# Levels one to five of a triangular inverse as 64-row by 64-column quarters of the array

## The chip, the cores and the metric

One core of one Trainium2 chip runs the whole program. The metric is the device time of one execution in microseconds.

## What is computed

The reference is a network of two blocks: a first block with a gated delta rule mixer (GDN), a sparse attention mixer and two feed-forward stages, then a second block with an mLSTM, a grouped attention and a mixture of experts. The change lies in the GDN mixer. What matters of it, cut from the reference:

```python
def gated_delta_rule_chunked(q, k, v, g, beta):
    ...
    gc = jnp.cumsum(g, axis=-1)
    decay = jnp.where(incl, jnp.exp(gc[..., :, None] - gc[..., None, :]), 0.0)
    L = jnp.where(strict, jnp.einsum('bhnid,bhnjd->bhnij', k * beta, k) * decay, 0.0)
    T = triangular_solve(eye + L, eye, lower=True, unit_diagonal=True)
    u = jnp.einsum('bhnij,bhnjd->bhnid', T, v * beta[..., None])
    w = jnp.einsum('bhnij,bhnjd->bhnid', T, kb * jnp.exp(gc)[..., None])
    ...
```

There are 256 tokens and 8 heads of width 128. T is the inverse of a unit lower triangular matrix.

## The kernel before, in words

The kernel works on chunks of 128 tokens, so for each of the 8 heads there are two 128x128 inverses. `gdn` (called by `mixer`) makes four generators `gdn_pair`, one for each pair of heads, and steps them in turn, each new pair `GAP` = 6 steps behind the last. A pair has four problems (two heads, two halves of the tokens), held side by side in tiles of [128, 4, 128].

A pair first projects its q, k, v columns (`ws2`, lines 356 to 358, with the splits of the weights into a high and a low half at lines 412 and 413). It then builds the negated strict lower part (`NL`, tile EL) and the start of the inverse and its transpose (`x`, tile X, and `ti`, tile T). Six levels follow, for block sizes s = 2, 4, 8, 16, 32, 64. Each level has five steps on a chain:

1. four matmuls `py` = NL times the even blocks of ti (line 936), 64 columns each,
2. a copy of py to `y` by ScalarE (line 937),
3. four matmuls `pz` = x times y (line 939),
4. a predicated copy of pz into the even blocks of ti by VectorE (line 941), under a mask `dm`,
5. four transposes of ti (line 944) and a copy to x by ScalarE (line 945).

A 128x64 fp32 matmul of the program is two passes in the trace, each with its own weight load, so a group of four is eight MATMUL rows; a transpose is one pass. Tiles py, pz and px come from one PSUM pool of four buffers, each a bank.

The program gives no order of its own: a scheduler places each instruction on its engine's queue by dependencies, priorities and its own estimate of durations, and puts the projection matmuls of other pairs (called dense below) between the steps of a chain. Each engine then runs its queue in that order. The projections use `acc` PSUM tiles, which are a pool of their own.

Behind the inverse come the state recurrence of the pair, the memory attention (`mem_attn`), the output projection, and the rest of the network. Two other places use part of the array already: the 64-row matmuls of the grouped attention (line 1444, two heads at rows 0 and 64) and a matmul of 64 rows by 64 columns (line 1254).

Of the kernel before, what the change touches and what calls it, by code (L numbers as in the profile page):

```python
# [14 lines left out]
AF = mybir.ActivationFunctionType  # L15
# [286 lines left out]
class Net:  # L302
# [549 lines left out]
    def gdn_pair(self, u, X, pool, sp, gc, gl, epsc, ahead):  # L852

        nc, I = self.nc, self.I
        hs = slice(2 * u, 2 * u + 2)
        t = lambda name, shape, bufs=2: pool.tile([128] + shape, F32, name=name, bufs=bufs)
        mm = nc.tensor.matmul
# [7 lines left out]
        for j in (1, 0, 2):  # L865
            p, = self.ws2(ahead.pop(0) if ahead else I["gqkv"][4 * j + u], X)
# [35 lines left out]
        NL = AT = None  # L902
        for kind, row, msk, other in (("L", rL, "mstrict", kC), ("A", rA, "mincl", qC)):
# [11 lines left out]
            NL, AT = (e, None) if kind == "L" else (NL, e)  # L915
        yield
        x, y, ti = t("X", [4, 128]), t("Y", [4, 64]), t("T", [4, 128])
# [7 lines left out]
        dm = self.dm.bitcast(I32).rearrange("p (i c) -> p i c", i=6)  # L925

        def blocks(tile, s, odd):
            return tile.rearrange("p h (n two s) -> p h n two s", two=2, s=s)[:, :, :, odd, :]

        for lv in range(1, 7):  # L930
            s = 1 << lv
            n = 64 // s
            cut = lambda z: z.rearrange("p h (n s) -> p h n s", s=s)
            py, pz = self.pst([128, 4, 64]), self.pst([128, 4, 64])
            for i in range(4):
                mm(cut(py)[:, i], NL[:, i, :], blocks(ti, s, 0)[:, i], start=True, stop=True)
            nc.scalar.activation(y, py, AF.Copy)
            for i in range(4):
                mm(pz[:, i, :], x[:, i, :], y[:, i, :], start=True, stop=True)
            mk = dm[:, lv - 1, :].rearrange("p (n s) -> p n s", s=s)[:, None].to_broadcast([128, 4, n, s])  # L940
            nc.vector.copy_predicated(blocks(ti, s, 0), mk, cut(pz))
            px = self.pst([128, 4, 128])
            for i in range(4):
                nc.tensor.transpose(px[:, i, :], ti[:, i, :], ident)
            nc.scalar.activation(x, px, AF.Copy)
            yield
# [29 lines left out]
        pz = self.xs2(I["gz"][u], X)  # L976
# [905 lines left out]
```

## Time and profile before

| | |
|---|---|
| three runs, median (lowest to highest) | 2262.7 us (2260.46 to 2262.75) |
| the profiled execution, its own time | 2260.96 us |
| its span, first to last instruction | 2258.9 us |
| TensorE (PE) busy, weight loads (PEld) busy | 1943.6 us, 1362.3 us |
| VectorE (DVE) busy, ScalarE (ACT) busy | 1058.1 us, 770.9 us |
| first and last row of the inverse's matmuls | 60.0 us, 255.1 us |

Times in the profile are microseconds from the first instruction unless marked ns. PE rows are matmuls, PEld rows the weight loads that go beside them; a row's duration overlaps with the next one's, so the pace is read from starts, not durations. The name left of the arrow is what is written, right of it what is read. "128*64 128x256" means 128 rows by 64 columns of weights, and 256 moving columns. A row of the timeline with "x8" stands for eight neighbours; its duration runs from the first one's start to the last one's end.

### The profile page before, as it was taken

To read this page: it belongs to the slowest core of one execution; us is meant where nothing else is said; L and a number is where in the kernel's file an instruction comes from. 1 tells how busy PE (TensorE), PEld (TensorE's weight loads), DVE (VectorE), ACT (ScalarE), POOL (GpSimd) and SP (SyncE) were. 2 spreads that over 40 slices of the span, in tenths; PEclk is the share of its full clock that TensorE was granted. 3 is DMA by queue.
4 is the path that set the end of the run, shared out by engine and by line. 5 is a ranking of instruction groups with operands and counts; after the bars stand their busy time and mean duration, and the time that the engine had idled before them with its cause. 6 is when DMAs were issued, how large, how long until landed. Compare 5 with 4: busy or idle time off the path is not lost. (4 is left out here: it accounts for less than half of the span.)

```text
span 2258.9 us, 31633 instructions
## 1 busy us (share of the span) xinstructions
PE 1943.6 (86%) x12918; PEld 1362.3 (60%) x12919; DVE 1058.1 (47%) x1899; ACT 770.9 (34%) x1336; POOL 99.7 (4%) x137
## 2 busy tenths in 40 slices
PE   8999999999999999999987666767999996667665
PEld 7999889988987998877942111112778831112121
DVE  6555378774546987876541111101875531111011
ACT  6476555444555444655410000000745410000000
POOL 0001000000000000211100000000020000000000
PEclk9999999999999999999998888777999998887877
DMA  6322267865525886545799999999555799999997
GB/s 229 122 101 77 87 265 297 313 264 176 186 75 211 328 335 240 174 145 234 283 378 420 421 420 421 420 420 387 199 219 227 258 411 421 420 420 421 421 389 329
DMA packets 96401, 653.16 MB, mean 289 GB/s; under 512 B 11592, under 2 KB 14832, under 8 KB 18680
## 3 DMA queue, kind: packets, MB, share of 16 engines
q1 hardware_dynamic: 96248, 651.05, 73.3%
q8 instruction: 105, 1.72, 0.3%
q14 instruction: 48, 0.39, 0.0%
HBM read 649.93 MB, written 1.08 MB: 288 GB/s over the span
## 5 line engine op out<-in xcount | busy, mean ns | idle before, releaser
L413 DVE TENSOR_TENSOR whl<-raw,whl 128x1024 fp32r<-128x1024 f32 x342 | 422.1, 1242 | 154.7 <-ACT whl L412 154.0
L412 ACT ACTIVATE whl<-raw 128x1024 fp32r<-128x1024 f32 x342 | 359.9, 1057 | 318.1 <-PE acc L358 149.1
L1681 PE MATMUL mm<-raw,q_XT 128*32 128x512 f32 x1808 | 273.0, 712 | 115.0 <-DMA raw<-in_moe 114.8
L1674 ACT ACTIVATE q_XT<-mm,mc,modA 128x128 f32<-128x128 f32 x64 | 29.3, 458 | 589.8 <-DVE q_XT L1676 348.8
L1681 PEld LDWEIGHTS mm<-raw,q_XT 128*32 128x32 f32 x1808 | 46.6, 117 | 303.9 <-DMA raw<-in_moe 180.1
L357 PE MATMUL acc<-xl,whl 128*128 128x256 f32 x784 | 227.4, 291 | 0.8 <-DVE xl L571 0.7
L356 PE MATMUL acc<-xh,whl 128*128 128x256 f32 x784 | 225.8, 290 | 2.0 <-ACT whl L412 1.8
L358 PE MATMUL acc<-xh,whl 128*128 128x256 f32 x784 | 224.9, 288 | 0.5 <-DVE whl L413 0.5
L358 PE MATMUL mm<-xh,whl 128*128 128x256 f32 x704 | 200.7, 285 | 1.4 <-DVE whl L413 1.4
L356 PE MATMUL mm<-xh,whl 128*128 128x256 f32 x704 | 201.5, 286 | 0.3
L357 PE MATMUL mm<-xl,whl 128*128 128x256 f32 x704 | 200.9, 285 | 0.3 <-DVE xl L571 0.3
L357 PEld LDWEIGHTS acc<-xl,whl 128*128 128x128 f32 x784 | 151.3, 193 | 4.5 <-issue 2.1
L356 PEld LDWEIGHTS acc<-xh,whl 128*128 128x128 f32 x784 | 150.9, 193 | 4.8 <-ACT whl L412 2.7
L358 PEld LDWEIGHTS acc<-xh,whl 128*128 128x128 f32 x784 | 150.9, 193 | 2.4 <-issue 1.3
L356 PEld LDWEIGHTS mm<-xh,whl 128*128 128x128 f32 x704 | 136.4, 194 | 3.9 <-issue 2.5
L358 PEld LDWEIGHTS mm<-xh,whl 128*128 128x128 f32 x704 | 136.5, 194 | 1.9 <-DVE whl L413 1.8
L357 PEld LDWEIGHTS mm<-xl,whl 128*128 128x128 f32 x704 | 136.5, 194 | 1.5 <-DVE xl L571 0.7
L1681 PE MATMUL mm<-raw,q_aT 128*32 128x512 f32 x592 | 83.2, 649 | 32.3 <-DMA raw<-in_moe 28.5
L1715 DVE TENSOR_TENSOR q_y<-mm,gate 128x512 f32<-128x512 f32 x32 | 22.1, 692 | 185.6 <-PE mm L1681 185.6
L1704 DVE TENSOR_TENSOR q_a<-q_a,mm 128x512 f32<-128x512 f32 x16 | 11.0, 688 | 204.2 <-PE mm L1681 204.2
L1208 DVE SCALAR_TENSOR_TENSOR adas<-adaw,cond,adas 128x2048 f32<-128x2048 f32 x42 | 98.5, 2346 | 5.7 <-DMA adaw<-in_ada 5.7
L1717 PE MATMUL acc<-q_y,q_WT 128*128 128x512 f32 x128 | 78.0, 741 | 22.8 <-DVE q_y L1715 22.0
(547 smaller groups left out, 3392.5 us busy)
## 6 DMA issues: line engine op xcount, KB each, us to landing
raw<-in_moe SPq DMA_DIRECT2D x300, 1024.0 KB, 19.9
raw<-in_ffn SPq DMA_DIRECT2D x66, 1024.0 KB, 5.9
whl<-in_moe SPq DMA_DIRECT2D x56, 1024.0 KB, 19.8
adaw<-in_ada SPq DMA_DIRECT2D x48, 1024.0 KB, 8.8
raw<-in_gmga SPq DMA_DIRECT2D x16, 1024.0 KB, 4.9
rawxh<-in_moe SPq DMA_DIRECT2D x14, 1024.0 KB, 19.8
rawxl<-in_moe SPq DMA_DIRECT2D x14, 1024.0 KB, 19.8
raw<-in_gqkv SPq DMA_DIRECT2D x12, 1024.0 KB, 8.5
```

What stands on the lines that cost most here:

```text
L356: mm(out, lh, rh, start=start, stop=False)
L357: mm(out, lh, rl, start=False, stop=False)
L358: mm(out, ll, rh, start=False, stop=stop)
L412: i = self.nc.scalar.activation(hi, src, AF.Copy)
L413: return i, self.nc.vector.tensor_sub(lo, src, hi.bitcast(F32))
L1208: nc.vector.scalar_tensor_tensor(a, t, c, a, op0=OP.mult, op1=OP.add)
L1674: nc.scalar.activation(XT[:, k, :], p, AF.Identity, bias=B[:, k:k + 1], scale=A[:, k:k + 1])
L1681: mm(out[s, :], lhs[:, s], ut[:, 512 * e:512 * e + 512], start=start, stop=stop, tile_position=(0, 32 * e))
L1704: nc.vector.tensor_mul(a, a, gu[1])
L1715: nc.vector.tensor_mul(y, p, gate[:, h * 512:h * 512 + 512])
L1717: mm(accs[tt][h], WT[:, tt, :], y, start=first, stop=last)
```

## The change

For levels one to five a block of the next size (up to 64) lies inside one of the two diagonal 64x64 quarters of the 128x128 matrix. The change computes only these: each of the four matmuls becomes two, one on rows and columns 0 to 63 of the array, one on 64 to 127, with half the moving columns (32). The upper quarter's products lie in the tile that was py, the lower one's in the tile that was pz; the first 32 columns of each hold the first product, the other 32 the second. The copy of the first product is one ScalarE copy for the upper half and one VectorE copy for the lower, and the predicated copy is one for each half. Level six is as before. The changed program's lines are 942 and 951 for the matmuls of the quarters, 948 (ScalarE) and 946 (VectorE) for the copies, 955 for the predicated copies, 958 to 963 for level six, 966 and 967 for the transposes and their copy.

```diff
--- before.py
+++ after.py
@@ -932,13 +932,35 @@
             n = 64 // s
             cut = lambda z: z.rearrange("p h (n s) -> p h n s", s=s)
             py, pz = self.pst([128, 4, 64]), self.pst([128, 4, 64])
-            for i in range(4):
-                mm(cut(py)[:, i], NL[:, i, :], blocks(ti, s, 0)[:, i], start=True, stop=True)
-            nc.scalar.activation(y, py, AF.Copy)
-            for i in range(4):
-                mm(pz[:, i, :], x[:, i, :], y[:, i, :], start=True, stop=True)
-            mk = dm[:, lv - 1, :].rearrange("p (n s) -> p n s", s=s)[:, None].to_broadcast([128, 4, n, s])
-            nc.vector.copy_predicated(blocks(ti, s, 0), mk, cut(pz))
+            even = blocks(ti, s, 0)
+            if lv < 6:
+
+                m = n // 2
+                halves = [(p, slice(64 * j, 64 * j + 64), slice(m * j, m * j + m)) for j, p in enumerate((py, pz))]
+                for i in range(4):
+                    for p, r, c in halves:
+                        mm(cut(p)[r, i, :m], NL[r, i, r], even[r, i, c], start=True, stop=True,
+                           tile_position=(r.start, r.start))
+                for p, r, c in halves:
+                    if r.start:
+                        nc.vector.tensor_copy(y[r, :, :32], p[r, :, :32])
+                    else:
+                        nc.scalar.activation(y[r, :, :32], p[r, :, :32], AF.Copy)
+                for i in range(4):
+                    for p, r, c in halves:
+                        mm(p[r, i, 32:], x[r, i, r], y[r, i, :32], start=True, stop=True,
+                           tile_position=(r.start, r.start))
+                for p, r, c in halves:
+                    mk = dm[r, lv - 1, r.start // 2:r.start // 2 + 32].rearrange("p (n s) -> p n s", s=s)
+                    nc.vector.copy_predicated(even[r, :, c], mk[:, None].to_broadcast([64, 4, m, s]), cut(p)[r, :, m:])
+            else:
+                for i in range(4):
+                    mm(cut(py)[:, i], NL[:, i, :], even[:, i], start=True, stop=True)
+                nc.scalar.activation(y, py, AF.Copy)
+                for i in range(4):
+                    mm(pz[:, i, :], x[:, i, :], y[:, i, :], start=True, stop=True)
+                mk = dm[:, lv - 1, :].rearrange("p (n s) -> p n s", s=s)[:, None].to_broadcast([128, 4, n, s])
+                nc.vector.copy_predicated(even, mk, cut(pz))
             px = self.pst([128, 4, 128])
             for i in range(4):
                 nc.tensor.transpose(px[:, i, :], ti[:, i, :], ident)
```

How the order moves. TensorE, first pair, level one. mm_550 and mm_551 are py and pz, whl the splits, cath and catl the input of the projection. Before, from the first group to the second:

```order
L936 MATMUL mm_550<-T_541,EL_508 128x64 x4
L357 MATMUL acc_638<-catl_90,whl_663 128x256
L358 MATMUL acc_638<-cath_89,whl_663 128x256
L356 MATMUL acc_638<-cath_89,whl_663 128x256
L357 MATMUL acc_638<-catl_90,whl_663 128x256
L358 MATMUL acc_638<-cath_89,whl_663 128x256
L356 MATMUL acc_638<-cath_89,whl_663 128x256
L939 MATMUL mm_551<-Y_540,X_539 128x64 x4
```

Now, at the same place, from the end of the first group (L942, where mm_550 and mm_551 alternate):

```order
L942 MATMUL mm_551<-T_541,EL_508 64x32
L357 MATMUL acc_648<-catl_90,whl_673 128x256
L358 MATMUL acc_648<-cath_89,whl_673 128x256
L356 MATMUL acc_648<-cath_89,whl_673 128x256
L357 MATMUL acc_648<-catl_90,whl_673 128x256
L951 MATMUL mm_551<-Y_540,X_539 64x32 x4
L358 MATMUL acc_648<-cath_89,whl_673 128x256
L356 MATMUL acc_648<-cath_89,whl_673 128x256
L951 MATMUL mm_550<-Y_540,X_539 64x32 x4
```

The second group has moved up by two dense matmuls, and it is in two pieces: all four matmuls of the lower quarter, two dense matmuls, all four of the upper quarter.

TensorE, second pair, level two, where the first group is in two pieces. Before:

```order
L966 MATMUL mm_1249<-vT_263,X_539 128x128
L936 MATMUL mm_1255<-T_1194,EL_1143 128x64 x4
L356 MATMUL acc_1444<-xh_127,whl_1469 128x256
L357 MATMUL acc_1444<-xl_128,whl_1469 128x256
L358 MATMUL acc_1444<-xh_127,whl_1469 128x256
```

Now:

```order
L988 MATMUL mm_1309<-vT_263,X_539 128x128
L942 MATMUL mm_1315<-T_1244,EL_1193 64x32 x4
L358 MATMUL acc_1524<-xh_127,whl_1521 128x256
...
L358 MATMUL acc_1524<-xh_127,whl_1549 128x256
L942 MATMUL mm_1316<-T_1244,EL_1193 64x32 x4
L356 MATMUL acc_1524<-xh_127,whl_1549 128x256
L357 MATMUL acc_1524<-xl_128,whl_1549 128x256
```

Between the two quarters of one group now stand ten dense matmuls.

VectorE, first pair, level one. Before:

```order
L914 SCALAR_TENSOR_TENSOR EA_528<-mm_533,EA_528 128x512
L413 TENSOR_TENSOR whl_753<-raw_751,whl_753 128x1024
L941 COPY_PREDICATED T_541<-k_dm_239,mm_551 128x128x2
L413 TENSOR_TENSOR whl_768<-raw_751,whl_768 128x1024
L413 TENSOR_TENSOR whl_785<-raw_783,whl_785 128x1024
```

Now:

```order
L914 SCALAR_TENSOR_TENSOR EA_528<-mm_533,EA_528 128x512
L946 COPY Y_540<-mm_551 64x4x32
L413 TENSOR_TENSOR whl_763<-raw_761,whl_763 128x1024
L955 COPY_PREDICATED T_541<-k_dm_239,mm_550 64x4x16x2
L955 COPY_PREDICATED T_541<-k_dm_239,mm_551 64x4x16x2
L413 TENSOR_TENSOR whl_778<-raw_761,whl_778 128x1024
```

The lower quarter's copy of Y, which waits for the first group, now stands ahead of a split, and one predicated copy has become two.

## Rows read from the trace of the kernel before

**Rows 1.** The page: its first line, and TensorE's granted clock in 40 equal slices

```profile
span 2258.9 us, 31633 instructions
...
PEclk9999999999999999999998888777999998887877
```

**Rows 2.** Busy time by stretch: PE, PEld, DVE, ACT, POOL busy us (x count), clock, DMA share, GB/s

```profile
100.00:125.00 25.00, 24.95 (x215) 24.28 (x215) 16.39 (x37) 17.81 (x32) 0.83 (x1) 1.00 0.32 119
150.00:175.00 25.00, 24.92 (x218) 24.62 (x216) 17.59 (x37) 20.04 (x32) 0.02 (x1) 1.00 0.45 142
```

**Rows 3.** Groups by line, 50 to 260 us (last row: all of L1278)

```profile
L939 PE MATMUL mm<-Y,X 128*128 128x64 f32 x192 | 25.1, 273 | 0.0
...
L945 ACT ACTIVATE X<-mm 128x512 f32<-128x512 f32 x24 | 14.3, 595 | 24.0 <-PE mm L944 23.6
L941 DVE COPY_PREDICATED T<-k_dm,mm 128x256 f32<-128x256 int32 x24 | 11.8, 492 | 30.1 <-PE mm L939 30.0
...
L937 ACT ACTIVATE Y<-mm 128x256 f32<-128x256 f32 x24 | 9.2, 385 | 9.2 <-PE mm L936 9.0
...
L1278 DVE COPY lac<-mm x2: 274/275/276, 943.7 to 1610.9; 128x128 f32<-128x128 f32 x2
```

**Rows 4.** Timeline of PE, a group without a wait: start us, us, instruction

```profile
132.16 0.28 PE L358 MATMUL acc<-xh,whl 128*128 128x256 f32 x1
132.28 1.00 PE L939 MATMUL mm<-Y,X 128*128 128x64 f32 x8
133.09 0.36 PE L356 MATMUL acc<-xh,whl 128*128 128x256 f32 x1
133.29 0.28 PE L357 MATMUL acc<-xl,whl 128*128 128x256 f32 x1
```

**Rows 5.** The same, the first and the last of 14 groups that wait

```profile
59.77 0.28 PE L356 MATMUL acc<-cath,whl 128*128 128x256 f32 x1
60.02 1.11 PE L936 MATMUL mm<-T,EL 128*128 128x64 f32 x8
...
61.14 0.28 PE L358 MATMUL acc<-cath,whl 128*128 128x256 f32 x1
...
249.06 0.28 PE L358 MATMUL acc<-xh,whl 128*128 128x256 f32 x1
249.35 1.10 PE L939 MATMUL mm<-Y,X 128*128 128x64 f32 x8
250.27 0.36 PE L356 MATMUL acc<-xh,whl 128*128 128x256 f32 x1
250.47 0.28 PE L357 MATMUL acc<-xl,whl 128*128 128x256 f32 x1
```

**Rows 6.** PE around a 64-row group; last row: its first weight loads (PEld)

```profile
1027.14 0.28 PE L358 MATMUL acc<-xh,whl 128*128 128x256 f32 x1
1027.35 1.13 PE L1444 MATMUL mm<-akC,aqC 64*128 64x256 f32 x8
1028.41 0.39 PE L356 MATMUL acc<-xh,whl 128*128 128x256 f32 x1
...
1027.34 0.19 PEld L1444 LDWEIGHTS mm<-akC,aqC 64*128 64x128 f32 x2
```

**Rows 7.** PE around the 64x64 group; its weight loads; its durations in ns, min/median/max

```profile
933.29 0.64 PE L1254 MATMUL mm<-li,consts 64*64 64x256 f32 x2
933.87 0.39 PE L358 MATMUL acc<-xh,whl 128*128 128x256 f32 x1
934.09 0.28 PE L356 MATMUL acc<-xh,whl 128*128 128x256 f32 x1
...
933.29 0.19 PEld L1254 LDWEIGHTS mm<-li,consts 64*64 64x64 f32 x2 [0.20 <-ACT li L1252]
...
L1254 PEld LDWEIGHTS mm<-li,consts x4: 129/130/133, 933.3 to 1599.1; 64*64 64x64 f32 x4
L1254 PE MATMUL mm<-li,consts x4: 376/402/427, 933.3 to 1599.3; 64*64 64x256 f32 x4
```

## The prediction, made before the changed kernel ran

> **What bounds the kernel now.** I read the page's slices first, then busy time by stretch, then the chain's groups by line, then single groups on the timeline. The levels of the inverse run between about 60 and 255 us of a span of 2258.9 us, and the granted clock is 1.00 there, the 2.4 GHz level [rows 1, 2]. TensorE is busy 24.9 of 25 us in that stretch and DVE 16 to 18 [rows 2]: the stage is bound by TensorE, which is filled with split-precision projection matmuls ("dense", one every 0.12 us) while the chains of the four head pairs run between them. DVE and ACT wait for TensorE there, not the other way: the predicated copy (L941) waited 30.0 us for L939, the X copy (L945) 23.6 us for L944 [rows 3]. So a microsecond of TensorE time saved or added in the stage moves everything behind it by one. What stands behind it needs the residual stream that this stage produces, and the order of instructions there is the same in both kernels.
>
> **What a group costs now.** Four 128-row matmuls of 64 columns are eight passes, each with its own weight load. One group without a wait: last dense matmul at 132.16, group at 132.28, next dense at 133.09 and 133.29 [rows 4]. That is 1.13 us where two dense steps would take 0.24, so the group costs 0.89 us; each pass takes 0.112, the pace of a 128-column weight load. Of the 48 groups, 27 lie directly between dense matmuls. 13 of these cost 0.89 to 0.93. 14 wait first for their operand and cost 1.14 on the mean; the first and the last of them are shown (61.14 - 59.77 - 0.24 = 1.13 and 250.47 - 249.06 - 0.24 = 1.17) [rows 5]. In these the group itself is longer too: 0.92 from its start to the next dense matmul, against 0.81, because the first weight load could not be pulled ahead of the wait. Mean of the 27: 1.02. The change removes 40 groups (levels one to five, two groups, four pairs): 40 x 1.02 = **40.8 us**, of which 35.6 is the clean price.
>
> **What a quarter costs.** No row of the trace runs two 64x64 quarters with 32 columns. The nearest are 64-row groups. (a) Going in: dense at 1027.14, first 64-row matmul at 1027.35, so 0.21 instead of 0.12 [rows 6]; the weight load starts with it and was not pulled ahead. (b) First load: in the one 64-row by 64-column group two loads, 0.13 us each, take 0.19 together, so the second starts 0.06 after the first [rows 7]. (c) Coming out: that group's second matmul starts at 933.29 + 0.64 - 0.376 = 933.55, its 256 columns stream for 0.21, and the next dense matmul starts at 933.87, 0.1 after the stream's end; the dense one after it comes 0.22 later, not 0.12 [rows 7]. 32 columns would stream in 0.03, so last matmul to dense is 0.12. (d) A step: half the columns of the full group's load, half of 0.112 = 0.056; the ends are 0.03 (only the 32 columns count, the load is hidden) and 0.112 (no gain from fewer columns). I take 0.056, as (b) is the row of the same shape, and keep the ends for the rivals. Two quarters do load together: two 64-row loads of 0.18 us lie within 0.19 [rows 6]. A run of n steps then costs 0.21 + 0.06 + (n - 1) x 0.056 + 0.12 + 0.22 - 0.24 = 0.31 + 0.056 n; with n = 8 that is 0.76, against 0.89. 40 whole runs would cost 30.4 us, 5 less than the clean 35.6.
>
> The order does not keep them whole. In the first group of a level the two quarters alternate in 14 of 20 cases; four others run one quarter after the other with dense work between, and two break off one matmul early. In the second group only 6 of 20 are whole: in the other 14 one quarter goes as soon as its own copy of Y is due, then dense matmuls, then the other quarter. A half run has four matmuls of one quarter, eight passes one behind the other, so eight steps: the full 0.76. Counted through the whole order there are 61 runs with 466 steps (40 runs with 320 if all were whole): 61 x 0.31 + 466 x 0.056 = 18.9 + 26.1 = **45.0 us**.
>
> The Trainium skill, TensorEngine Tiling (Array Packing), section Key Properties, says that changing the tiling mode drains the engine; the 0.09 us in (a) and the 0.1 in (c) agree. The same page's section Theoretical Speedup gives up to 2x for a dimension of 64 or less; by it alone the 40 groups would halve, 17.8 us less, 2245, which is the first rival below.
>
> **Waits.** Of the 0.25 us that a waiting group costs more, 0.11 is the unhidden load, which a run has anyway (its 0.06), and up to 0.09 of the rest passes while the array drains. About 0.06 stays, on half of 40: 1.2 us. Y is copied by ACT and DVE side by side, 128 columns each: by the slope between 0.385 (256 columns) and 0.595 (512) an ACT copy is 0.28, a DVE copy of 128 columns 0.275 [rows 3], so 0.1 less per level. The predicated copy becomes two on the same engine, each between half of 0.49 and the whole; near 0.31 with the fixed part that these copies have, so 0.13 more per level [rows 3]. 20 levels: +0.6, hidden where dense work stands between; I take 0, bounds -2 and +3. DVE gets 20 x (0.275 + 0.62 - 0.49) = 8 us more work, which fits beside its 50 to 70% [rows 2]. But the Y copy on DVE waits for TensorE with a split (L413) queued behind it, whose low half TensorE itself needs; the split buffers are four deep, so I cost that at nothing, and at 5 us if that cover is gone. PSUM buffers: the same three per level, the first held until the predicated copy instead of the Y copy; within the same bounds. No DMA moves.
>
> **Sum.** 45.0 + 1.2 - 40.8 = **+5.4 us**. On the profiled execution (2260.96 us, with 2.1 us outside its span) that is 2266.4. The median of the three runs is 2262.7, 1.7 above it, and they spread over 2.3; on the median it is **2268.1**, which I give.
>
> **Rivals.** (1) The quarters pay. If going in and out cost nothing, the steps alone would be 466 x 0.056 = 26 us: 15 us less, 2248. It turns faster where the fixed part of a run is below 0.16 us (61 x 0.16 + 26.1 = 36, 4.5 under 40.8), or where a step is near 0.03 (18.9 + 14 = 33, 8 under). For it: more array in use. Against: both ways of the switch are seen [rows 6, 7], with the same prices. 0.04. (2) No change that shows: steps at 0.053, runs that end at transposes (whose identity loads faster) and no waits left, since a run takes longer and the copies are done: 45 - 2 + 0 - 40.8 = +2, 2265. For it: the switch hides waits. Against: it needs all of these at once, or a good part of them. 0.27. (3) Much slower: the two quarters do not load together, so that the 22 alternating runs take 16 steps, 22 x 8 x 0.056 = +10, 2278 (a step of 0.112 throughout would give +26, 2294); or DVE, blocked by its Y copies, starves TensorE of splits, +5 and more, 2273 to 2278. Against: loads side by side [rows 6] and the four buffers. 0.09. That the change does not do what it says is partly true already (half runs) and stands in the sum.
>
> **Numbers.** 0.2% (4.5 us) is about what a measurement of this kernel can tell from no change. My forecast, +4.5 to +9.5, has 0.60. With the third rival slower has 0.69, same 0.27, faster 0.04. The range, 2262.5 to 2275, takes in the bounds of the waits (-2, +3) and most of the second rival, and leaves out the first and most of the third.
>
> **What would show it.** TensorE busy as before between 60 and 255 us, and the last transposes of level six (L966) some 5 us later than 255. Between a dense matmul and the first quarter 0.21, from the last quarter matmul to the next dense 0.12, then 0.22; passes of one quarter 0.056 apart. Half runs of about 0.76 in excess. DVE busy some 8 us more. Wrong if quarter passes follow at less than 0.04 or at 0.11, if dense matmuls follow a quarter at their usual pace, or if TensorE shows new waits for the splits.

## The result and the profile after

| | before | changed |
|---|---|---|
| median of the runs (lowest to highest) | 2262.62 us (2260.46 to 2262.75) | 2274.07 us (2271.74 to 2278.85) |
| ratio, 95% interval | | 1.0053 (1.0036 to 1.007) |
| the profiled execution, its span | 2258.9 us | 2269.9 us |

The change made the kernel slower by 11.5 us on the medians; 5.4 was forecast, and the range to 2275 just holds the time. The same kernel measured once more, below, came to 2276.4, outside it.

The page of the changed kernel, its first line and the granted clock in 40 slices, to set beside [rows 1]:

```profile
span 2269.9 us, 32342 instructions
...
PEclk9999999999999999999998787877999997877778
```

Slices of 57 us hide what happened in the stage of the inverse. By stretches of 5 us (length; PE, PEld, DVE, ACT, POOL busy us; granted clock, DMA share, GB/s), the changed kernel:

```profile
100.00:105.00 5.00, 5.00 (x53) 4.60 (x53) 2.97 (x6) 0.59 (x2) 0.00 (x0) 0.89 0.47 192
105.00:110.00 5.00, 5.00 (x48) 4.32 (x46) 2.50 (x6) 3.97 (x6) 0.00 (x0) 0.77 0.01 3
...
245.00:250.00 5.00, 5.00 (x63) 4.46 (x61) 2.92 (x6) 2.28 (x4) 1.27 (x2) 1.00 0.00 0
250.00:255.00 5.00, 4.67 (x41) 3.72 (x40) 1.63 (x7) 3.33 (x5) 0.00 (x0) 0.91 0.01 3
255.00:260.00 5.00, 5.00 (x34) 4.61 (x34) 1.29 (x3) 1.50 (x4) 0.00 (x0) 0.50 0.00 0
260.00:265.00 5.00, 5.00 (x37) 4.71 (x37) 1.82 (x3) 1.51 (x2) 0.00 (x0) 0.57 0.20 25
```

The kernel before, in one of these stretches:

```profile
255.00:260.00 5.00, 4.98 (x37) 4.42 (x35) 0.00 (x0) 3.80 (x9) 0.04 (x1) 1.00 0.00 0
```

TensorE is still busy nearly all the time, so the stage is still bound by it. But it ran at the lower level (0.50, 1.2 GHz) for (0.11 + 0.23) x 5 / 0.5 = 3.4 us near 104 and for (0.09 + 0.50 + 0.43) x 5 / 0.5 = 10.2 us up to 264, where the kernel before had 1.00. That is 6.8 us of work lost, which the prediction did not foresee.

The groups by line, 50 to 270 us, beside [rows 3]; L942 and L951 are the quarters, L946 and L948 the copies of Y, L955 the predicated copies:

```profile
L951 PE MATMUL mm<-Y,X 64*64 64x32 f32 x320 | 23.2, 227 | 0.0
...
L942 PE MATMUL mm<-T,EL 64*64 64x32 f32 x320 | 17.2, 228 | 0.3
...
L955 DVE COPY_PREDICATED T<-k_dm,mm 64x128 f32<-64x128 int32 x40 | 13.0, 325 | 19.1 <-PE mm L951 14.2 <-ACT whl L412 2.4 <-issue 1.3
...
L946 DVE COPY Y<-mm 64x128 f32<-64x128 f32 x20 | 5.9, 294 | 29.7 <-PE mm L942 29.6
...
L948 ACT ACTIVATE Y<-mm 64x128 f32<-64x128 f32 x20 | 5.4, 269 | 4.3 <-PE mm L942 4.1
```

The copies cost what was estimated (0.269 for 0.28, 0.294 for 0.275, 0.325 for 0.31), and still the copies wait for TensorE. How a half run and a whole run look in the changed kernel, on the timeline of PE (start us, us, instruction), to set beside [rows 4]:

```profile
236.18 0.28 PE L358 MATMUL acc<-xh,whl 128*128 128x256 f32 x1
236.38 0.65 PE L951 MATMUL mm<-Y,X 64*64 64x32 f32 x8
236.96 0.39 PE L356 MATMUL acc<-xh,whl 128*128 128x256 f32 x1
237.18 0.28 PE L357 MATMUL acc<-xl,whl 128*128 128x256 f32 x1
...
247.69 0.28 PE L357 MATMUL acc<-xl,whl 128*128 128x256 f32 x1
247.90 0.66 PE L951 MATMUL mm<-Y,X 64*64 64x32 f32 x16
248.50 0.39 PE L358 MATMUL acc<-xh,whl 128*128 128x256 f32 x1
248.72 0.28 PE L356 MATMUL acc<-xh,whl 128*128 128x256 f32 x1
```

One pass is 0.22 us long (tile Y, instructions on PE; ns min/median/max, then first and last start):

```profile
L951 PE MATMUL mm<-Y,X x320: 219/219/313, 61.5 to 261.3; 64*64 64x32 f32 x160
```

The half run, eight passes of one quarter, costs 237.18 - 236.18 - 0.24 = 0.76 us; the whole run, sixteen passes of both, costs 248.72 - 247.69 - 0.24 = 0.79. So the second quarter is free when it goes beside the first (0.66 against 0.65 for the runs themselves), and a run that holds one quarter alone costs as much as one that holds both.

Where the time went is best read at a place behind the inverse at which both kernels do the same, the first L564 matmul on PE. Before, then changed:

```profile
305.87 0.60 PE L564 MATMUL acc<-diag,xres 128*128 128x128 f32 x4
```

```profile
320.20 0.60 PE L564 MATMUL acc<-diag,xres 128*128 128x128 f32 x4
```

The stage ends 14.3 us later. The same way of counting as above (second matmul behind a run, minus the last one before it, minus 0.24), summed over every run of the levels one to five, gives 50.0 us for the 61 runs of the changed kernel and 38.2 us for the 40 full groups before (46.2 for all 48, 8.0 of it level six): 11.9 more. Five runs lie at the low clock and took 6.6 us where five clean ones take 3.9. The other 6.8 - 2.7 = 4.1 us of lost clock fell on dense matmuls and transposes. Together 16.0; the remaining -1.7 is not traced to a place. Between 306 and 600 us 4.3 us come back. The kernel before had two low stretches there of 0.34 x 5 / 0.5 = 3.4 us each, which cost it 1.7 us of work each, and the changed one had none; that would be 3.4 of the 4.3 (kernel before, by stretch):

```profile
470.00:475.00 5.00, 2.73 (x23) 1.69 (x22) 5.00 (x8) 2.21 (x3) 0.00 (x0) 1.00 0.57 179
475.00:480.00 5.00, 5.00 (x30) 4.93 (x31) 3.82 (x4) 0.00 (x0) 0.00 (x0) 0.66 0.80 317
560.00:565.00 5.00, 3.89 (x67) 3.36 (x67) 0.93 (x3) 1.22 (x3) 0.19 (x1) 0.66 0.99 369
```

### The profile page after: what moved, and what is told of

It is laid out like the page before. It is cut to its first block, busy times and chain, and to the rows that moved or that the text cites. A ratio compares the mean times of both kernels' runs of the same rounds, so it can differ in the third digit from the quotient of the medians.

```text
span 2269.9 us, 32342 instructions
## 1 busy us (share of the span) xinstructions
PE 1969.6 (87%) x13238; PEld 1368.2 (60%) x13239; DVE 1067.9 (47%) x1939; ACT 768.2 (34%) x1336; POOL 94.3 (4%) x137
## 5 line engine op out<-in xcount | busy, mean ns | idle before, releaser
L1703 PE MATMUL mm<-raw,q_XT 128*32 128x512 f32 x1808 | 284.1, 737 | 110.2 <-DMA raw<-in_moe 110.1
L1723 DVE COPY q_WT<-mm 128x256 f32<-128x256 f32 x16 | 6.8, 423 | 195.6 <-PE mm L1721 195.6
```

The lines of the kernel that those rows point to most:

```text
L1703: mm(out[s, :], lhs[:, s], ut[:, 512 * e:512 * e + 512], start=start, stop=stop, tile_position=(0, 32 * e))
L1723: nc.vector.tensor_copy(WT, pt)
```

## The experiments

The theory: the quarters are cheap as such, and the change loses by how they are cut into runs. Each quarter has a PSUM tile of its own, so each becomes ready by its own copy, and the order sends it alone. Rivals: the evacuation (copies on two engines, two predicated copies), the PSUM buffers, the bank itself, and the clock.

In the table, runs are the pieces that the order makes of the 40 groups of levels one to five, the sum is that of their prices in the profile, counted as above, and L564 is when the first of these matmuls starts. Each ratio is to the kernel before in the same set of runs; its medians in the three sets are in the first row.

| kernel | runs | sum, us | L564 at, us | median, us | ratio (95%) |
|---|---|---|---|---|---|
| before | 45 | 38.2 | 305.9 | 2262.5 to 2263.4 | |
| changed | 61 | 50.0 | 320.2 | 2274.1 | 1.0053 (1.0036 to 1.0070) |
| changed, once more | 61 | 50.1 | 322.7 | 2276.4 | 1.0065 (1.0050 to 1.0080) |
| one_bank_split | 42 | 32.8 | 300.7 | 2252.6 | 0.9953 (0.9940 to 0.9967) |
| one_bank | 43 | 32.8 | 300.0 | 2254.3 | 0.9965 (0.9952 to 0.9978) |
| act_both | 49 | 39.5 | 311.4 | 2261.8 | 0.9992 (0.9981 to 1.0004) |
| full_evac | 45 | 37.6 | 305.2 | 2263.1 | 1.0002 (0.9992 to 1.0013) |
| one_bank_serial | 43 | 42.6 | 310.9 | 2267.3 | 1.0018 (1.0007 to 1.0029) |
| shared_two | 43 | 32.8 | 300.7 | 2252.4 | 0.9960 (0.9945 to 0.9975) |
| one_pred | 45 | 34.1 | 302.3 | 2255.8 | 0.9970 (0.9960 to 0.9980) |
| by_problem | 60 | 40.4 | 310.8 | 2259.7 | 0.9985 (0.9975 to 0.9996) |
| four_first | 52 | 35.4 | 300.8 | 2255.3 | 0.9968 (0.9957 to 0.9980) |

### Both quarters in one PSUM tile

```diff
-            py, pz = self.pst([128, 4, 64]), self.pst([128, 4, 64])
+            py = self.pst([128, 4, 64])
+            pz = py if lv < 6 else self.pst([128, 4, 64])
```

The upper quarter's products go to partitions 0 to 63 of the tile, the lower one's to 64 to 127. Nothing else differs from the change: two copies of Y on two engines, two predicated copies.

> Both quarters write one PSUM tile (upper one partitions 0 to 63, lower one 64 to 127); copies on ScalarE and VectorE and the predicated copies are as in the change. In the order the quarters now stay together: 42 runs instead of 61. Theory (the number of runs is what is wrong with the change; each measured 0.77 us): 42 x 0.77 = 32.5 us against 40.8 for the 40 full groups and 47.3 for the 61 runs at full clock; with 1 us of waits about 7 us under the kernel before, 2255, and 2253 to 2260 as the clock falls. Rival A (two quarters in one bank do not go side by side, 16 steps): 42 x 1.2 = 50 us, 9 over before, 2272, and passes of the quarters 0.05 apart in place of pairs 0.01 apart. Rival B (quarter runs bring the clock down, and that is where the time goes): shorter runs, but still low-clock stretches between 60 and 265 us, 2262 to 2266.

Measured: 2252.6 us, 10 us under the kernel before and 21 under the change. A second group on PE of this kernel:

```profile
133.46 0.28 PE L358 MATMUL acc<-xh,whl 128*128 128x256 f32 x1
133.67 0.66 PE L952 MATMUL mm<-Y,X 64*64 64x32 f32 x16
134.25 0.39 PE L356 MATMUL acc<-xh,whl 128*128 128x256 f32 x1
134.48 0.28 PE L357 MATMUL acc<-xl,whl 128*128 128x256 f32 x1
```

All 20 second groups are whole now, and a whole run in one bank takes 0.66 us as in two: rival A falls. The copies are the same as in the change, by the groups by line of this kernel:

```profile
L956 DVE COPY_PREDICATED T<-k_dm,mm 64x128 f32<-64x128 int32 x40 | 13.1, 326 | 15.1 <-PE mm L952 14.5
...
L947 DVE COPY Y<-mm 64x128 f32<-64x128 f32 x20 | 5.9, 295 | 10.8 <-ACT Y L949 10.3
L949 ACT ACTIVATE Y<-mm 64x128 f32<-64x128 f32 x20 | 5.4, 268 | 5.1 <-PE mm L943 4.8
```

So the change loses by the cutting, and by the low clock in its stage, which this profile does not have (1.00 in every stretch from 55 to 300 us). The sum of the runs fell by 5.4 us against before, and L564 comes 5.2 earlier. The span is 7.7 shorter (2251.2): the rest lies behind L564, where this profile has no low stretch at 475 or 560.

### One copy of Y

```diff
-                for p, r, c in halves:
-                    if r.start:
-                        nc.vector.tensor_copy(y[r, :, :32], p[r, :, :32])
-                    else:
-                        nc.scalar.activation(y[r, :, :32], p[r, :, :32], AF.Copy)
+                nc.scalar.activation(y[:, :, :32], py[:, :, :32], AF.Copy)
```

On top of the tile shared by both quarters.

> As one_bank_split, but Y is copied by one ScalarE instruction (128 partitions, 128 columns). 43 runs. Theory (evacuation is hidden behind dense work): within 2 us of one_bank_split, about 2255. Rival (VectorE's Y copies, 20 x 0.29 us, and its waits with splits queued behind cost time): 3 to 6 us faster than one_bank_split.

2254.3 against 2252.6, the intervals overlap: VectorE's copies cost nothing that shows here. The rival falls.

### The change with both copies of Y on ScalarE

```diff
                 for p, r, c in halves:
-                    if r.start:
-                        nc.vector.tensor_copy(y[r, :, :32], p[r, :, :32])
-                    else:
-                        nc.scalar.activation(y[r, :, :32], p[r, :, :32], AF.Copy)
+                    nc.scalar.activation(y[r, :, :32], p[r, :, :32], AF.Copy)
```

> As the change, two banks, but both Y copies on ScalarE. The order has 49 runs: 32 whole, 14 half runs, 3 others. Theory (runs decide): 49 x 0.77 = 37.7 us, 9.6 under the change's 47.3, 3 under before plus 1 of waits: 2260 to 2264. Rival (VectorE's copies are the cost): 2255 or less. Rival B (clock): 2266 to 2270, with low clock in the stage.

2261.8, inside the theory's 2260 to 2264, with 49 runs and 39.5 us. Each quarter still has its own tile and its own copy, but the copies end one behind the other on one engine, and the order splits fewer groups. One low stretch lies in its stage too (0.73 between 120 and 125 us), and one ahead of it (0.56 and 0.75 in the two stretches from 50 to 60 us): its first group starts at 63.55, that of the kernel before at 60.02. That is 3.5 of the 5.5 us by which its L564 comes later.

### Full groups with the change's evacuation

```diff
-            nc.scalar.activation(y, py, AF.Copy)
+            if lv < 6:
+                nc.scalar.activation(y[:64], py[:64], AF.Copy)
+                nc.vector.tensor_copy(y[64:], py[64:])
+            else:
+                nc.scalar.activation(y, py, AF.Copy)
...
+                for r, c in ((slice(0, 64), slice(0, m)), (slice(64, 128), slice(m, n))):
+                    mk = dm[r, lv - 1, r.start // 2:r.start // 2 + 32].rearrange("p (n s) -> p n s", s=s)
+                    nc.vector.copy_predicated(even[r, :, c], mk[:, None].to_broadcast([64, 4, m, s]), cut(pz)[r, :, c])
```

> Full 128-row groups as in the kernel before, but the copy of Y in two halves (ScalarE, VectorE) and the predicated copy in two halves, for levels one to five. Theory (evacuation is hidden): -1 to +2 us against before, 2262 to 2265. Rival (the two-engine copies and the second predicated copy lengthen the chains): +4 to +6, 2267 to 2269. No low clock between 60 and 265 us if the quarters are what brings it down.

2263.1, no change (1.0002), and the clock was 1.00 from 60 to 265 us. Its two Y copies even took longer than the change's (0.375 and 0.428 us, 256 columns each), and the extra work still hid.

### The quarters one behind the other

```diff
-                for i in range(4):
-                    for p, r, c in halves:
+                for p, r, c in halves:
+                    for i in range(4):
```

In both groups, on top of one_bank.

> As one_bank, but within a group all four matmuls of the upper quarter come first, then the four of the lower, so that neighbours in the queue use the same quarter. 43 runs as in one_bank, with 16 steps instead of 8. Theory (pairs of passes go side by side only where neighbours use different quarters; a step is 0.057 us): a run costs 0.21 + 15 x 0.057 + 0.15 + 0.22 - 0.24 = 1.20 us, 43 x 0.43 = 18 us over one_bank, about 2272. Rival (the two quarters overlap whatever their order, or the entry and exit are all that counts): within 4 us of one_bank, 2251 to 2258.

2267.3, some 12 us over one_bank by the ratios (1.0018 and 0.9965): between the two. A run on PE of this kernel, and below it how many of its passes lie in two stretches of it, begun or still running (length; busy us of PE, of PEld):

```profile
134.26 0.28 PE L358 MATMUL acc<-xh,whl 128*128 128x256 f32 x1
134.47 0.91 PE L948 MATMUL mm<-Y,X 64*64 64x32 f32 x16
135.31 0.39 PE L356 MATMUL acc<-xh,whl 128*128 128x256 f32 x1
135.53 0.28 PE L357 MATMUL acc<-xl,whl 128*128 128x256 f32 x1
```

```profile
134.46:134.71 0.25, 0.24 (x4) 0.24 (x5) 1.00 0.00 0
134.71:134.95 0.24, 0.24 (x11) 0.24 (x9) 1.00 0.00 0
```

The run costs 135.53 - 134.26 - 0.24 = 1.03, not 1.20. The run of 0.91 is 0.25 longer than the interleaved one, four steps and not eight: at first only one quarter works, then both for a time (4 passes in the first stretch; 11 in the second, 3 of them begun in the first). In the trace the starts come in pairs from the fifth pass on, at 134.72 and 134.73. So TensorE did start the second quarter while passes of the first stood ahead of it in the queue, but only when some four of them were left. Passes of different quarters overlap within a short stretch of the queue. The order of issue counts, though less than I had expected.

### A tile for each product, shared by both quarters

```diff
-            py = self.pst([128, 4, 64])
-            pz = py if lv < 6 else self.pst([128, 4, 64])
+            py, pz = self.pst([128, 4, 64]), self.pst([128, 4, 64])
...
-                        mm(p[r, i, 32:], x[r, i, r], y[r, i, :32], start=True, stop=True,
+                        mm(pz[r, i, :32], x[r, i, r], y[r, i, :32], start=True, stop=True,
```

> As one_bank, but the second products go to a PSUM tile of their own again (three tiles for each level as in the change and before; both quarters share each). 43 runs. Theory (runs stay whole because both quarters wait for one tile): 43 x 0.77 = 33 us, as one_bank, 2252 to 2256. Rival (one_bank is fast because a level takes two PSUM buffers instead of three): back to 2260 or more.

2252.4: the third PSUM buffer for a level costs nothing. What counts is that both quarters share a tile, not how many tiles there are.

### One predicated copy again

```diff
-                for r, c in halves:
-                    mk = dm[r, lv - 1, r.start // 2:r.start // 2 + 32].rearrange("p (n s) -> p n s", s=s)
-                    nc.vector.copy_predicated(even[r, :, c], mk[:, None].to_broadcast([64, 4, m, s]), cut(pz)[r, :, :m])
+                mk = dm[:, lv - 1, :].rearrange("p (u n s) -> p u n s", u=2, s=s)[:, None].to_broadcast([128, 4, 2, m, s])
+                nc.vector.copy_predicated(even.rearrange("p h (u n) s -> p h u n s", u=2), mk,
+                                          cut(pz)[:, :, None, :m].to_broadcast([128, 4, 2, m, s]))
```

On top of shared_two.

> As shared_two, and the predicated copy is one instruction again (the 32 columns read twice, the mask picks the right half). 45 runs. Theory (evacuation is hidden): same as shared_two within 2 us. Rival (the second predicated copy is on the path of the chains): 3 us or more under shared_two.

2255.8, overlapping with shared_two and not faster: the rival falls. One instruction of 0.50 us takes the place of two of 0.33. This profile has a low stretch in the stage too (0.67 between 210 and 215 us).

### The changed kernel once more

> The changed kernel once more, for its granted clock by stretch. Theory (stretches of low clock of 3 us and more come in any of these kernels somewhere between 55 and 600 us, and are not tied to a place): not at 104 and at 254 to 264 us again; the inverse's stage then ends 6 to 9 us behind the kernel before instead of 14, and the time stays within 2270 to 2279. Rival (quarter runs bring the clock down at these places): low clock again within 5 us of 104 and of 254, and 14 us lost by 306 us.

A miss for the theory, at one of the two places. 2276.4 (1.0065, 1.0050 to 1.0080). Near 104 the clock was 1.00, but the end of the stage was slow again, and longer (second profile of the changed kernel, by stretch):

```profile
250.00:252.00 2.00, 1.83 (x14) 1.33 (x14) 0.80 (x4) 0.81 (x3) 0.00 (x0) 1.00 0.04 8
252.00:254.00 2.00, 2.00 (x19) 1.57 (x18) 0.58 (x2) 1.99 (x3) 0.00 (x0) 0.82 0.00 0
254.00:256.00 2.00, 2.00 (x13) 1.91 (x13) 0.30 (x1) 0.47 (x1) 0.00 (x0) 0.50 0.00 0
...
266.00:270.00 4.00, 4.00 (x21) 4.00 (x21) 0.45 (x1) 0.24 (x1) 0.00 (x0) 0.50 0.48 203
270.00:275.00 5.00, 5.00 (x42) 4.84 (x41) 1.23 (x1) 4.53 (x10) 0.00 (x0) 0.97 0.02 3
```

L564 came at 322.7. The low stretch at the end of the stage is seen in both profiles of the change, and in no other kernel's profile here. Low stretches elsewhere in the stage are seen in act_both, by_problem and one_pred, one profile each, and in neither kernel with full groups.

What went before it both times is a thin piece: in 250 to 252 us the weight loads were busy for 1.28 and 1.33 of 2 us, seven and six quarter runs lay within 246 to 254 us, and TensorE stood still for 0.33 and 0.17 us. The low stretches of the kernel before follow thin pieces too (2.73 of 5 us busy between 470 and 475, 4.18 of 5 between 555 and 560). But a thinner piece of the changed kernel was followed by full clock. Its first profile, that piece and the one ahead of the low stretch:

```profile
204.00:206.00 2.00, 1.37 (x14) 1.15 (x14) 1.78 (x6) 1.35 (x3) 0.18 (x1) 1.00 0.00 0
250.00:252.00 2.00, 1.67 (x14) 1.28 (x13) 0.99 (x4) 0.69 (x2) 0.00 (x0) 1.00 0.04 8
```

And the clock fell near 104 us although TensorE was busy without a break from 100 to 105. So it is not shown that the quarter runs bring the clock down, nor what does: no run changed the fill of one piece alone.

### Split by problem instead of by quarter

```diff
-                halves = [(p, slice(64 * j, 64 * j + 64), slice(m * j, m * j + m)) for j, p in enumerate((py, pz))]
+                halves = [(slice(64 * j, 64 * j + 64), slice(m * j, m * j + m)) for j in range(2)]
+                bank = (py, py, pz, pz)
...
+                nc.scalar.activation(y[:, :2, :32], py[:, :2, :32], AF.Copy)
+                nc.vector.tensor_copy(y[:, 2:, :32], pz[:, 2:, :32])
```

Matmuls of problem i, both quarters, write bank[i].

> Two PSUM tiles for each level again, but split by problem: both quarters of problems 0 and 1 in one, of problems 2 and 3 in the other; Y copied by ScalarE (0, 1) and VectorE (2, 3), four predicated copies of 64 columns. 60 runs, nearly as many as in the change, but a broken group holds both quarters, so a half run has four steps, not eight. Theory (a run costs 0.34 us and 0.057 for each step, and pairs go side by side): 19 whole runs at 0.78, some 33 halves at 0.55, 8 others at 0.6, 38 us, 5 over one_bank, about 2259 (2256 to 2263). Rival (the number of times the array is entered decides): as the change, 2271 or more.

2259.7, with nearly as many runs as the change (60 for 61) and 14 us faster. A half run with both quarters in it:

```profile
105.91 0.28 PE L358 MATMUL acc<-xh,whl 128*128 128x256 f32 x1
106.12 0.42 PE L949 MATMUL mm<-Y,X 64*64 64x32 f32 x8
106.48 0.39 PE L356 MATMUL acc<-xh,whl 128*128 128x256 f32 x1
106.70 0.28 PE L357 MATMUL acc<-xl,whl 128*128 128x256 f32 x1
```

It costs 106.70 - 105.91 - 0.24 = 0.55, against 0.76 for the half run of one quarter. So it is both things in the change: 0.3 us for each entry and exit, and steps in which half of what could work stands idle. Its sum is 40.4 where 38 was expected; a low stretch up to 70 us (0.75 and 0.57 in the two stretches from 60 on), which put 1.6 us on three runs, explains most of that.

### Four quarters at a time

The first products of problems 2 and 3 go to the other half of the partitions, in a tile of their own, and are copied back across:

```diff
+                            o = r if i < 2 else (lo if r is up else up)
+                            mm(cut(p)[o, i, :m], NL[r, i, r], even[r, i, c], start=True, stop=True,
+                               tile_position=(r.start, o.start))
...
+                nc.scalar.activation(y[up, 2:, :32], pz[lo, 2:, :32], AF.Copy)
+                nc.scalar.activation(y[lo, 2:, :32], pz[up, 2:, :32], AF.Copy)
+                nc.scalar.activation(y[:, :2, :32], py[:, :2, :32], AF.Copy)
```

> First products of a level on all four 64x64 quarters of the array (problems 2 and 3 written to the other half of the partitions, in a second PSUM tile, and copied back across by ScalarE, which makes three copies of Y), second products as in one_bank. 52 runs, 15 of the first groups whole. Theory (four quarters go side by side too: starts of four passes within 0.03 us and 0.057 to the next four, 0.55 us for a whole first group): sum of runs about 32 us, as one_bank, 2251 to 2257. Rival (only two at a time, 0.78 for a whole first group): 36 us, 2256 to 2261.

2255.3, no better than one_bank. Four do go side by side: a whole first group of sixteen passes takes 0.43 us here instead of 0.66. But the second product now finds its operands late; one such group in the same kernel waits inside the run, at 0.85 instead of 0.66:

```profile
101.88 0.43 PE L945 MATMUL mm<-T,EL 64*64 64x32 f32 x16
102.25 0.39 PE L357 MATMUL acc<-xl,whl 128*128 128x256 f32 x1
102.47 0.28 PE L358 MATMUL acc<-xh,whl 128*128 128x256 f32 x1
```

```profile
99.62 0.85 PE L952 MATMUL mm<-Y,X 64*64 64x32 f32 x16
100.40 0.39 PE L356 MATMUL acc<-xh,whl 128*128 128x256 f32 x1
100.62 0.28 PE L357 MATMUL acc<-xl,whl 128*128 128x256 f32 x1
```

The third copy of its Y ends at 100.01, inside the run:

```profile
99.79 0.22 ACT L948 ACTIVATE Y<-mm 64x64 f32<-64x64 f32 x1
```

Of the 16 second groups that stayed whole, 12 cost 0.92 to 1.03 us, where a whole run of the others costs 0.78. Three copies of 0.22 us one behind the other take the place of one of 0.28, and the two tiles split first groups again (52 runs). What the steps gave, the waits and the splits took.

## Why the prediction was right, and where it was not

- **What bounds the stage**: right. TensorE stayed full, and the time of L564 moves with the sum of the runs: -5.4 gave -5.2 in one_bank_split, -0.6 gave -0.7 in full_evac, +4.4 gave +5.0 in one_bank_serial, +11.9 and 4.1 of clock gave +14.3 in the change. In act_both and by_problem L564 came 4.2 and 2.7 us later than the sum says, in four_first 2.3 earlier. Much of that lies ahead of the stage: its first group starts at 60.02 in the kernel before, at 63.55, 62.03 and 59.00 in these three. Counted from the first group, L564 moves by +2.0, +3.0 and -4.0 for sums of +1.3, +2.2 and -2.8 (by -5.4 for -5.4 in one_bank_split, +4.4 for +4.4 in one_bank_serial). The first two have low clock within the stage; the 1.2 left in four_first are unexplained.
- **The order**: right. 61 runs, in both profiles, and with 42 runs the change turns into a gain.
- **The price of a run**: right. 0.76 was forecast; 0.76 and 0.79 are seen, of which going in is 0.20 to 0.21. Coming out is 0.15 where 0.12 was taken (236.96 - 236.38 - 0.65 + 0.22, a pass being 0.22 long), and the steps 0.02 less than taken. Sum at full clock 50.0 - 2.7 = 47.3, forecast 45.0 and 1.2 of waits.
- **The price of the full groups**: wrong, 40.8 for 38.2. The failing step was to take the mean of the 27 groups between dense matmuls, 1.02, for all 40. The other 21 groups stand beside transposes and other small matmuls and cost 0.88 each (46.2 - 27.6 = 18.5 us), and nearly all of them found their operand ready. This is 2.6 us of the miss.
- **The clock**: missing in the sum. [rows 2] showed 1.00 throughout the stage and I held it for given. It cost 6.8 us in the stage, 2.7 of it in the runs. Against the kernel before, some 3.4 us came back later, as two low stretches of that kernel were absent here. Why the clock fell in the stage stays open.
- **Waits and evacuation**: right to cost them at nothing (full_evac, one_bank, one_pred), and the split buffers held.
- **The range**: held in part by luck. In the stage the change lost 14.3 us, not 5.4; 4.3 of it came back behind the stage, for no reason that the prediction gives. The second measurement lies outside.
- **The rivals**: the first, quarters that pay, is false for this change, but true for the same quarters in one tile. It was put down to entry and exit that cost nothing; they cost what I had said, and the gain came from keeping the runs whole: 0.78 is less than the 0.89 of a full group. My own figure of 30.4 us for 40 whole runs was beside 40.8 in the text, and 32.8 was measured. The third rival's step of 0.112 and its blocked VectorE did not come. One sum of the first rival is off, to no effect: 61 x 0.16 + 26.1 is 35.9, which is 4.9 under 40.8, not 4.5.

A full group is entered 0.12 us behind the last dense matmul and left 0.08 behind the start of its own last pass (132.28 + 1.00 - 0.27 = 133.01, a pass being 0.27 long [rows 3, 4]); a run of quarters, in each of these kernels, 0.20 to 0.21 and 0.15. The Trainium skill, TensorEngine Tiling (Array Packing), section Key Properties, says that a change of the tiling mode drains the engine; these two differences agree. The 0.22 that follows, which the prediction's (c) counts to coming out, is no sign of the change of mode: behind a full group the second dense matmul comes after 0.20 too [rows 4]. So of the 0.31 that the prediction gives each run beside its steps, about 0.18 (0.09 + 0.07 + 0.02, an estimate from these rows) comes with the quarters; a full group pays the like of the rest.

## What to carry to other kernels

When a matmul is cut into pieces that run beside each other, make them ready at the same time: let them share the tile that they write, so that the scheduler keeps them together; a piece that goes alone pays the whole price of entering and leaving. Then check the order for how many runs there are, and interleave the pieces within each. Price what is removed group by group by what stands next to it, not by the mean of the groups that are easiest to read.

## What was not expected of the hardware

- Quarters that write different partitions of the same PSUM bank ran side by side as fast as with a bank each (0.66 us for sixteen passes in both).
- Four 64x64 quarters ran side by side, sixteen passes in 0.43 us against 0.66 for two at a time.
- With the quarters issued one behind the other, the second one started before the first was through: 0.91 us, where sixteen passes in a row would take about 15 x 0.061 + 0.22 = 1.14, with (0.65 - 0.22) / 7 = 0.061 for a step.
- TensorE fell to 1.2 GHz for 10 and 17 us at the end of the stage in the two profiles of the change, with PE busy 4.67 and 4.83 of the 5 us from 250 on; behind 204 to 206 us, where PE was busy for 1.37 of 2, the clock of the first stayed at 1.00.
